# Joined blocks behind the first and third norm of a DeepNorm layer, and an eleventh pair of weights with its sums made ahead

## The chip, the cores and the metric

One core of one Trainium2 chip. The metric is device microseconds (us) from start to end of one execution. The trace is that of one profiled execution; its times are us from the start of its span. TensorE is PE, VectorE is DVE, ScalarE is ACT, GpSimd is POOL, SyncE is SP.

## The reference

One layer on 256 tokens of width 2048, all in float32:

```
h = layer_norm(alpha*x + 0.5*swiglu(x, w_ffn1_gu, w_ffn1_down))          # norm i=0
rq, rk, rv, rg, aq, ak, av, gate_r, gate_a = split(h @ w_in)
ret_branch = (silu(rg) * group_norm(retention(rot(rq), rot(rk), rv))) @ w_ret_out
att_branch = sliding_window_attention(rot(aq), rot(ak), av, sinks) @ w_att_out
mixed = (sigmoid(gate_r)*ret_branch + sigmoid(gate_a)*att_branch) @ w_mix_out
h = layer_norm(alpha*h + mixed)                                          # norm i=1
h = layer_norm(alpha*h + 0.5*swiglu(h, w_ffn2_gu, w_ffn2_down))          # norm i=2
ple = sigmoid(h @ w_ple_gate) * (p @ w_ple_proj)
return layer_norm(alpha*h + ple)                                         # norm 3
swiglu(x, w_gu, w_down) = (silu(x @ w_g) * (x @ w_u)) @ w_down           # inner width 5632
```

## The kernel before, in words

**Products.** Every float32 operand is split into a high part (a cast by ScalarE, L105) and a low part (the difference, by VectorE, L106). A product of two such operands is three matmuls: `Sum.add` issues low x high (L431), high x high (L432) and high x low (L433), each with 128 x 128 weights on 512 columns. Weights come from memory in chunks of 512 KB (256 rows of the product by 512 columns): a load on SyncE's queue (L119) into a tile `r...`, then `h...` and `l...`. A chunk gives two k-steps for both halves t of the 128 tokens, 12 matmuls. All these tiles come from one pool of slots. A planner (`plan`, `fill`) keeps a list of the chunks in the order of their use, and loads and splits each as far ahead as slots and a budget of queued TensorE time allow. Each engine, and SyncE's queue, works in the order in which the program was written.

**Units.** A pair of chunks of the two feed-forward products (gate/up) can be worked in several ways, named by a letter in a string per group of 512 columns (`gu_units`, L937): P is plain, 24 matmuls; F is plain with the low part of one of the chunks accumulated by a transfer on POOL's queue (L170); S is a unit of seven products in place of eight, as Strassen's, 21 matmuls, for which VectorE makes four sums (L226 to L229) and three splits; D is the same unit with its sums `u` and `v` made and split ahead and put in memory, from where they are loaded when needed (`Prepared`). `AHEAD` says which pairs of the second feed-forward part are D: ten pairs, in groups 1, 2, 3, 4, 5 and 7.

`sums_ahead` (L275) makes these sums, as a generator: for each pair two loads, four adds on VectorE (L294, L295, L298, L299), two casts on ScalarE (L297, L301), two differences on VectorE (L304, L306) and four stores on SyncE's queue. `run_side` (L366) is called behind each chunk on TensorE: it runs the next job of the list `side` (to which `later(n, job)` adds a job n calls ahead), and one step of the first generator in `slow` and of the first in `lazy`.

**Norm and turn.** Behind each norm the 256 x 2048 result (tiles `f1y`, `mixy`, `f2y`, in four quarters of 512 columns for each half t of the tokens) has to be turned, since the next product needs it by columns (tile `ht`). `ln_turn` does it on TensorE: four 128 x 128 transposes (L693) into `lnps`, a cast (L105) and a difference (L106). `Norm.first` (L809) is called with the first chunks of the next product. It multiplies these for t=0, holding them, and then again for t=1 (this is the held front), while a list of events says after which chunk (counted through both passes) which quarter (t, c) is normalised or turned. Behind the first norm the front is six chunks of block 0 of the retention's values (`rv`), and behind the third, six of block 0 of the embedding's gate (`pg`). The order is written out by hand.

The middle norm does two things otherwise: its front joins two blocks (three pairs of chunks each for both, `FRONT_PAIRS`), and its quarter 3 is turned by a transfer, the class `Turn`: ScalarE copies the quarter's 32-bit words as two planes of 16 bits (`part`, L185), SyncE issues a transposing transfer (`move`, L189), and ScalarE joins the planes again (`join`, L196) before the usual cast and difference. `by_transfer` names the quarters that go this way.

**Stages around the change.** Norm 0; `rv` block 0; features of the retention's queries and keys (`rqk`, L382), beside them the angle tables (`slow`) and the sums ahead; `rv` blocks 1 to 3; `rg`; attention features and, as jobs of `side`, attention (scores L1412, softmax L1417 to L1453, transposing transfers); beside these jobs the four gates `gt`, then the Strassen part of the other gate (`ga0`, `ga1`); the branches, mixing (two more pairs of sums), norm 1, the second feed-forward part, norm 2, the four blocks `pg`, and norm 3 on their sums. Behind each `pg` block `finish` makes the sigmoid (L1632), the product with `ppr` (L1634), the sum with the residual (L1635) and its statistics (L1636).

Of the kernel before, what the change touches and what calls it, by code (L numbers as in the profile page):

```python
# [8 lines left out]
F32 = mybir.dt.float32  # L9
F32R = mybir.dt.float32r  # L10
# [30 lines left out]

SEVEN = (0, 1, 2, 3)

AHEAD = {1: (4, 5), 2: (4,), 3: (4, 5), 4: (4,), 5: (4, 5), 7: (4, 5)}
AHEAD_SLOTS = 36

DELAY = 1
# [15 lines left out]
def layer(ctx: ExitStack, tc: tile.TileContext, io):  # L63
# [13 lines left out]
    def banks(name):  # L77
        return [bank(name + str(j)) for j in range(2)]
# [266 lines left out]
    def take(key):  # L345
        if not ready:
            fill(True)
        u = ready.pop(0)
        assert u.key == key, (u.key, key)
        return u  # L350

    def done(u):
        room["used"] -= u.keeps
        fill()

    def slots_for_weights(n, ahead=45, far=90):
        room.update(slots=n, ahead=ahead, far=far)
# [825 lines left out]
    ret_keys = lambda b: lambda n, p: ("w_ret2", 4 * b + 2 * n, p)  # L1183

    def plan_mixers():
        plan_tokens(("w_rv", 0), KD)
        for grp in range(8):
            plan_features([("w_in_f", grp)], KD)
        for blk in range(1, 4):
            plan_tokens(("w_rv", blk), KD)  # L1190
        for grp in range(8, 16, 2):
            plan_tokens(("w_in_f2", grp), KD)
        plan_tokens(("w_av",), KD, nk=4)
        for grp in (20, 16, 17, 18, 19):
            plan_features([("w_in_f", grp)], KD)
        for grp in range(21, 29, 2):
            plan_tokens(("w_in_f2", grp), KD)
        for b in range(2):
            block_units(GATE_UNITS, gate_keys(b))
        for j in range(0, 8, 2):  # L1200
            plan_tokens(("w_att2", j), KD // 2)
        for b in range(2):
            block_units(RET_UNITS[b], ret_keys(b))
        block_units(MIX_UNITS, mix_keys)
        for blk in range(2, 4):
            plan_tokens(("w_mix", blk), KD)

    def later(n, job):
        for j in range(n):
            if len(side) <= j:  # L1210
                side.append(idle)
        side.insert(n, job)

    def mixers(ht, norm, residual, keepers, away):
# [24 lines left out]
        def values(blk, ps):  # L1239
            hi, lo = (slot([P, 2, 512], F32R, f"rv{w}{blk}") for w in "hl")  # L1240
            for t in range(2):
                split(hi[:, t], lo[:, t], ps[t])
            rv.append((hi, lo))

        ps = banks("rv0")
        sums = [[Sum(ps[t], KD)] for t in range(2)]
        norm.first([(("w_rv", 0, c), 2 * c, 0) for c in range(FRONT)], rhs, sums, (
            (5, (1, 0)), (6, (1, 1)), (8, (1, 2)), (8, "more"), (9, (1, 3)), (10, (0, 3)), (10, "go"),
        ))
        slots_for_weights(24)  # L1250
        for c in range(FRONT, KD // 2):
            u = take(("w_rv", 0, c))
            tokens_chunk(u.chunk, 2 * c, rhs, [sums[t][0] for t in range(2)], (0, 1))
            done(u)
        values(0, ps)
        slots_for_weights(14)
        ahead = [(gu_keys("f2", j)(0, p), gu_keys("f2", j)(1, p)) for j in AHEAD for p in AHEAD[j]]
        def angles():
# [3 lines left out]

        slow.append(angles())
        lazy.append(sums_ahead(ahead[:3], 3, 2))
        lazy.append(sums_ahead(ahead[3:8], 2, 2))
        for grp in range(8):
            ps = banks(f"rqk{grp}")
            features_out([(("w_in_f", grp), ps)], KD, both_halves)
# [2 lines left out]
        decay = [slot([P, 2, 384], F32, f"dec{j}") for j in range(4)]  # L1271
        for j in range(4):
            act.dma_start(decay[j], io["decay"][:, 2 * j : 2 * j + 2, :])
        for blk in range(1, 4):
            ps = banks(f"rv{blk}")
            tokens_out(("w_rv", blk), KD, rhs, ps)
            values(blk, ps)
# [225 lines left out]

        made = {}
        forms = lambda p: made[p // 2](p % 2)
        slots_for_weights(18)
        sig = []
        for j in range(4):
# [76 lines left out]

        lhs = lambda k: of_pairs(mix_t, k)
        slots_for_weights(16)
        lazy.append(sums_ahead(ahead[8:], 3, 2))

        def residual_added(blk, ps):  # L1590
            for t in range(2):
# [33 lines left out]
    def embedding(ht, norm, y):  # L1625
# [36 lines left out]
        def scale(blk):  # L1662
            sl = y[blk][:, 1]
            dve.tensor_tensor(sl, sl, g[blk // 2][:, blk % 2 * 512 : blk % 2 * 512 + 512], ALU.mult)
            v = slot([P, 2, 512], F32R, f"yg{blk}")
            split(v[:, 0], v[:, 1], sl)
            scaled[blk] = v
# [43 lines left out]
                sync.dma_start(out[:, blk * 512 : blk * 512 + 512], sl)  # L1711

        lhs = lambda k: (ht[:, k, :S], ht[:, k, S:])
        for blk in range(4):
            pgs = banks(f"pg{blk}")
            sums = [Sum(b, KD) for b in pgs]
            sg = slot([P, 2, 512], F32, f"sg{blk}")
            key = ("w_pg", blk)
            if blk == 0:
                for j in range(4):  # L1720
                    pp[j] = load_columns(pp, j, "ppr")
                steps = [(key + (c,), 2 * c, 0) for c in range(FRONT)]
                norm.first(steps, lhs, [[s] for s in sums], (
                    (1, (0, 2)), (1, "sums"), (5, (1, 0)), (6, (1, 1)), (7, (1, 2)), (7, "more"), (8, (1, 3)),
                    (9, (0, 3)), (10, "go"),
                ))
                slots_for_weights(24)
                for c in range(FRONT, KD // 2):
                    u = take(key + (c,))
                    tokens_chunk(u.chunk, 2 * c, lhs, sums, (0, 1))  # L1730
                    done(u)
            elif blk < 3:
                for c in range(KD // 2):
                    u = take(key + (c,))
                    tokens_chunk(u.chunk, 2 * c, lhs, sums, (0, 1))
                    done(u)
                    run_side()
            if blk < 3:
                finish(blk, pgs[0], sg, 0)
                later(1, lambda blk=blk, pgs=pgs, sg=sg: finish(blk, pgs[1], sg, 1))  # L1740
                if blk == 0:
                    g, b = ln_vectors(3)
                    two_rows = small.tile([P, 96], F32, tag="plnm", bufs=1, name="plnm")
                    pool.memset(two_rows, 0.0)
                    ident_r = small.tile([P, P], F32R, tag="identr", bufs=1, name="identr")
                    act.copy(ident_r, ident)
                if blk == 1:
                    later(3, rows_of_vectors)
                    later(4, lambda: scale(0))
                    later(6, lambda: scale(1))  # L1750
                if blk == 2:
                    later(6, lambda: scale(2))
# [55 lines left out]
    with tc.manual_schedule():  # L1808
        dve.memset(warm, 0.0)
        for eps, v in roots.items():  # L1810
            dve.memset(v, 4.0 * eps)
        act.activation(warm, warm, AF.Silu)
        plan_ffn("f1")
        plan.extend(Single(("w_pp", blk, 0)) for blk in range(2))
        plan_mixers()
        plan.extend(Single(("w_pp", blk, 0)) for blk in range(2, 4))
        plan_ffn("f2")
        for blk in range(4):
# [108 lines left out]
```

## Time and profile before

| what | us |
|---|---|
| median of three runs | 2230.26 (2229.8 to 2233.0) |
| the profiled execution, its own time | 2231.88 |
| its span, first to last instruction | 2230.0 |
| TensorE busy | 2220.2 |
| VectorE busy | 1999.0 |
| ScalarE busy | 1429.3 |

The granted TensorE clock is 0.999 on average. A row of the timeline has start, duration, engine, line, operation, output <- inputs and in brackets the idle time ahead of it with what ended it; rows of the same line in succession are put together (x4). A row of the windows has the stretch, its length, for each engine its busy time and instructions, and at the end the granted clock, the mean share of the DMA engines and GB/s. A group has its busy time and mean ns behind the bar. Matmuls overlap, so the duration of one (390 ns) is no price; the distance between the starts is.

### The profile page before, as it was taken

The numbers are of one execution on the slowest core, as the hardware profiler recorded it, in microseconds if no ns is written. First come the engines' busy times: TensorE is split into PE (matmuls) and PEld (weight loads), VectorE is DVE, ScalarE is ACT, GpSimd is POOL, SyncE is SP. The second block draws the span as 40 slices with busy tenths as digits, with TensorE's granted clock in tenths as the row PEclk, the third lists the DMA queues.
The fourth block names the chain that finished last, engine by engine and source line by source line (L and its number), as shares of the span: only waits on it lengthen the run. The fifth ranks groups of instructions, "written<-read, shape, count | busy, mean of one in ns | idle before, by whom it ended". The sixth has DMA issues, their size and how long they took to land.

```text
span 2230.0 us, 29094 instructions
## 1 busy us (share of the span) xinstructions
PE 2220.2 (100%) x10159; PEld 1841.2 (83%) x10159; DVE 1999.0 (90%) x2619; ACT 1429.3 (64%) x1670; POOL 51.9 (2%) x66
## 2 busy tenths in 40 slices
PE   9999999999999999999999999999999999999998
PEld 8888888888888888888788888888888888888887
DVE  6999999989988898889789888779999999999977
ACT  6777777776565445557766467466667677765633
POOL 0000000000000000000000000000000000000000
PEclk9999999999999999999999999999999999999999
DMA  9989998976686989846756578788898999676871
GB/s 323 254 259 257 250 258 249 263 225 217 230 306 255 324 297 320 268 172 208 208 166 240 176 210 323 302 302 274 304 299 269 297 249 276 205 237 224 300 272 68
DMA packets 296363, 565.01 MB, mean 253 GB/s; under 512 B 94348, under 2 KB 98828, under 8 KB 296216
## 3 DMA queue, kind: packets, MB, share of 16 engines
q1 hardware_dynamic: 286024, 530.68, 71.3%
q0 software_dynamic: 8208, 29.89, 7.2%
q10 hardware_dynamic: 1984, 2.58, 0.3%
q8 instruction: 80, 1.31, 0.2%
q14 instruction: 67, 0.55, 0.1%
HBM read 484.43 MB, written 29.36 MB: 230 GB/s over the span
## 4 chain that ended last, share of the span: by engine, by line
PE 94%; DVE 2%; DMA 2%; issue 1%; ACT 0%; SPq 0%; ACTq 0%; POOL 0%; DVEq 0%; POOLq 0%
PE f2g L432 3%; PE f2g L431 3%; PE f2g L433 3%; PE rqk L382 3%; PE f1g L433 2%; PE f1g L431 2%; PE f1g L432 2%; PE f2u L432 2%; PE f2u L431 2%; PE f2u L433 2%; PE f1u L433 2%; PE f1u L431 2%; PE f1u L432 2%; PE aqk L382 2%; PE f2e L431 1%; PE f2e L432 1%
## 5 line engine op out<-in xcount | busy, mean ns | idle before, releaser
L106 DVE TENSOR_TENSOR lf_gu<-rf_gu,hf_gu 128x1024 fp32r<-128x1024 f32 (+1 forms) x225 | 267.6, 1210 | 23.7 <-ACT hf_gu L105 22.7
L105 ACT CAST hf_gu<-rf_gu 128x1024 fp32r<-128x1024 f32 (+1 forms) x225 | 228.6, 1039 | 25.8 <-DMA rf_gu<-in_f_gu 21.8
L106 DVE TENSOR_TENSOR lw_in_f<-rw_in_f,hw_in_f 128x1024 fp32r<-128x1024 f32 x140 | 167.6, 1219 | 18.6 <-ACT hw_in_f L105 18.4
L106 DVE TENSOR_TENSOR lf_down<-rf_down,hf_down 128x1024 fp32r<-128x1024 f32 x130 | 155.7, 1219 | 14.1 <-ACT hf_down L105 13.3
L105 ACT CAST huf_gu<-uf_gu 128x1024 fp32r<-128x1024 f32 x76 | 80.1, 1054 | 122.7 <-DVE uf_gu L227 104.0
L105 ACT CAST hf_down<-rf_down 128x1024 fp32r<-128x1024 f32 x130 | 132.6, 1048 | 31.2 <-DMA rf_down<-in_f_down 21.3
L105 ACT CAST hw_in_f<-rw_in_f 128x1024 fp32r<-128x1024 f32 x140 | 140.9, 1049 | 9.0 <-DMA rw_in_f<-in_w_in_f 4.0
L105 ACT CAST hvf_gu<-vf_gu 128x1024 fp32r<-128x1024 f32 x76 | 80.1, 1054 | 31.6 <-DVE vf_gu L229 29.3
L106 DVE TENSOR_TENSOR luf_gu<-uf_gu,huf_gu 128x1024 fp32r<-128x1024 f32 x76 | 92.6, 1218 | 0.0
L106 DVE TENSOR_TENSOR lvf_gu<-vf_gu,hvf_gu 128x1024 fp32r<-128x1024 f32 x76 | 92.5, 1218 | 0.0
L431 PE MATMUL f1g<-hf_gu,xt 128*128 128x512 f32 x232 | 90.7, 391 | 0.0
L432 PE MATMUL f1g<-hf_gu,xt 128*128 128x512 f32 x232 | 90.5, 390 | 0.0
L433 PE MATMUL f1g<-lf_gu,xt 128*128 128x512 f32 x232 | 90.4, 390 | 0.0
L431 PE MATMUL f2g<-hf_gu,ht 128*128 128x512 f32 x214 | 83.3, 389 | 0.0
L433 PE MATMUL f2g<-lf_gu,ht 128*128 128x512 f32 x214 | 83.3, 389 | 0.0
L432 PE MATMUL f2g<-hf_gu,ht 128*128 128x512 f32 x214 | 83.3, 389 | 0.0
L170 POOL DMA_DIRECT2D lf_gu<-rf_gu x43 | 37.4, 869 | 1640.7 <-PE f2u L433 980.9
L433 PE MATMUL f1u<-lf_gu,xt 128*128 128x512 f32 x192 | 74.9, 390 | 0.5 <-DMA lf_gu<-rf_gu 0.5
L431 PE MATMUL f1u<-hf_gu,xt 128*128 128x512 f32 x192 | 74.7, 389 | 0.0
L432 PE MATMUL f1u<-hf_gu,xt 128*128 128x512 f32 x192 | 74.7, 389 | 0.0
L105 ACT CAST huf_down<-uf_down 128x1024 fp32r<-128x1024 f32 x32 | 33.7, 1053 | 60.0 <-DVE uf_down L227 58.7
L431 PE MATMUL f2u<-hf_gu,ht 128*128 128x512 f32 x168 | 65.6, 391 | 0.0
(1498 smaller groups left out, 6921.5 us busy)
## 6 DMA issues: line engine op xcount, KB each, us to landing
rf_gu<-in_f_gu SPq DMA_DIRECT2D x360, 512.0 KB
rf_down<-in_f_down SPq DMA_DIRECT2D x176, 512.0 KB
rw_in_f<-in_w_in_f SPq DMA_DIRECT2D x148, 512.0 KB
lf_gu<-rf_gu POOLq DMA_DIRECT2D x43, 512.0 KB, 7.9
rw_rv<-in_w_rv SPq DMA_DIRECT2D x32, 512.0 KB
rw_ret<-in_w_ret SPq DMA_DIRECT2D x32, 512.0 KB
rw_mix<-in_w_mix SPq DMA_DIRECT2D x32, 512.0 KB
rw_pg<-in_w_pg SPq DMA_DIRECT2D x32, 512.0 KB
```

What stands on the lines that cost most here:

```text
L105: act.copy(dst_hi, src)
L106: (lo_engine or dve).tensor_tensor(dst_lo, src, dst_hi, ALU.subtract)
L170: pool.dma_start(c.lo, c.raw, accum_op=ALU.add)
L382: pe.matmul(ps[f], hi[:, kk, f * P : (f + 1) * P], rhs(k), start=k == 0, stop=k == n_k - 1,)
L431: pe.matmul(o, al, bh, start=first, stop=False)
L432: pe.matmul(o, ah, bh, start=False, stop=False)
L433: pe.matmul(o, ah, bl, start=False, stop=self.left == 0)
```

## The change

1. `AHEAD` gets `6: (4,)`: group 6 of the second feed-forward part goes from `PFSSFSSP` to `PFSSDSSP`. Eleven pairs have their sums made ahead: three and then three (five before) beside `rqk`, `rv` and `rg`, three in the gates (new), two in the mixing as before.
2. Behind norm 0, blocks 0 and 1 of `rv` are joined: the held front is three pairs of chunks for both blocks, the other five pairs follow with `run_side` behind each chunk, and block 1 no longer comes behind `rqk`.
3. Behind norm 2, blocks 0 and 1 of `pg` are joined in the same way. Their finishes become jobs of `side` in block 2, and the preparations for norm 3 (`rows_of_vectors`, `scale`) go behind them.
4. At both places quarter 3 is turned by a transfer and joined by a job of `side`, one call behind the front; the lists of events are written anew.

```
-AHEAD = {1: (4, 5), 2: (4,), 3: (4, 5), 4: (4,), 5: (4, 5), 7: (4, 5)}
+AHEAD = {1: (4, 5), 2: (4,), 3: (4, 5), 4: (4,), 5: (4, 5), 6: (4,), 7: (4, 5)}
...
-        ps = banks("rv0")
-        sums = [[Sum(ps[t], KD)] for t in range(2)]
-        norm.first([(("w_rv", 0, c), 2 * c, 0) for c in range(FRONT)], rhs, sums, (
-            (5, (1, 0)), (6, (1, 1)), (8, (1, 2)), (8, "more"), (9, (1, 3)), (10, (0, 3)), (10, "go"),
-        ))
+        pv = [banks(f"rv{n}") for n in range(2)]
+        sums = [[Sum(pv[n][t], KD) for n in range(2)] for t in range(2)]
+        norm.by_transfer = 3,
+        norm.first(
+            [(("w_rv", n, p), 2 * p, n) for p in range(FRONT_PAIRS) for n in range(2)], rhs, sums, (
+                (5, (1, 0)), (6, (1, 1)), (7, (1, 2)), (7, "more"), (8, (0, 3)), (8, (1, 3)), (9, ("move", 3)), (10, "go"),
+            )
+        )
+        later(1, lambda: norm.join(3))
         slots_for_weights(24)
-        for c in range(FRONT, KD // 2):
-            u = take(("w_rv", 0, c))
-            tokens_chunk(u.chunk, 2 * c, rhs, [sums[t][0] for t in range(2)], (0, 1))
-            done(u)
-        values(0, ps)
+        for p in range(FRONT_PAIRS, KD // 2):
+            for n in range(2):
+                u = take(("w_rv", n, p))
+                tokens_chunk(u.chunk, 2 * p, rhs, [sums[t][n] for t in range(2)], (0, 1))
+                done(u)
+                run_side()
+        for blk in range(2):
+            values(blk, pv[blk])
...
         lazy.append(sums_ahead(ahead[:3], 3, 2))
-        lazy.append(sums_ahead(ahead[3:8], 2, 2))
+        lazy.append(sums_ahead(ahead[3:6], 2, 2))
...
-        for blk in range(1, 4):
+        for blk in range(2, 4):
             ps = banks(f"rv{blk}")
...
+        lazy.append(sums_ahead(ahead[6:9], 2, 2))
         slots_for_weights(18)
...
-        lazy.append(sums_ahead(ahead[8:], 3, 2))
+        lazy.append(sums_ahead(ahead[9:], 3, 2))
...
+        norm.first(
+            [(("w_pg", n, p), 2 * p, n) for p in range(FRONT_PAIRS) for n in range(2)], lhs, sums, (
+                (1, "sums"), (4, (0, 2)), (5, (1, 0)), (6, (1, 1)), (7, "more"), (8, (1, 2)), (8, (0, 3)), (9, (1, 3)), (10, ("move", 3)), (10, "go"),
+            )
+        )
+        later(1, lambda: norm.join(3))
...
+        for blk in range(2):
+            finish_later(2 * blk, blk, pair[blk], gates[blk])
...
+        later(4, rows_of_vectors)
+        later(5, lambda: scale(0))
+        later(6, lambda: scale(1))
```

The order of the instructions shows what moves. First TensorE at the end of the held front behind norm 0, before (`rv01` is block 0 for t=1, `lnps0112` and `lnps0012` are quarter 3 for t=1 and t=0):

```order
L433 MATMUL rv01_6129<-lw_rv_0_2_5900,ht0_5955 128x512
L693 MATMUL lnps0112_6228<-ident_72,f1y3_5591 128x128 x4
L431 MATMUL rv01_6129<-hw_rv_0_3_5917,ht0_5955 128x512
L432 MATMUL rv01_6129<-hw_rv_0_3_5917,ht0_5955 128x512
L433 MATMUL rv01_6129<-lw_rv_0_3_5918,ht0_5955 128x512
```

The same place of the change, behind the last group of transposes that is left (quarter 2 for t=1, `lnps018`; `rv11` is block 1 for t=1):

```order
L433 MATMUL rv01_6129<-lw_rv_0_0_5864,ht0_5955 128x512
L693 MATMUL lnps018_6209<-ident_72,f1y2_5545 128x128 x4
L431 MATMUL rv11_6131<-hw_rv_1_0_5881,ht0_5955 128x512
L432 MATMUL rv11_6131<-hw_rv_1_0_5881,ht0_5955 128x512
L433 MATMUL rv11_6131<-lw_rv_1_0_5882,ht0_5955 128x512
```

Both groups of quarter 3 are gone, quarter 2's group stands behind the first held chunk of the second pass and not behind a later one, and each chunk alternates with one of block 1. In all TensorE has 16 transposes and 3 matmuls fewer.

ScalarE at the end of the same front, before (`hw_rv_0_6` is the high part of chunk 6 of block 0):

```order
L105 CAST ht0_5955<-lnps018_6213 128x4x128
L105 CAST ht0_5955<-lnps0112_6228 128x4x128
L105 CAST ht0_5955<-lnps0012_6241 128x4x128
L105 CAST hw_rv_0_6_6254<-rw_rv_0_6_5952 128x1024
L105 CAST hw_rv_0_7_6258<-rw_rv_0_7_5962 128x1024
```

And of the change (`wln03`, `mln03` and `lnr03` are quarter 3 as planes, turned, and joined; `few` is a table's first use):

```order
L105 CAST ht0_5955<-lnps018_6209 128x4x128
L185 COPY wln03_6224<-f1y3_5591 128x1024 x2
L105 CAST hw_rv_0_3_6247<-rw_rv_0_3_5952 128x1024
L105 CAST hw_rv_1_3_6251<-rw_rv_1_3_5962 128x1024
L105 CAST hw_rv_0_4_6255<-rw_rv_0_4_6054 128x1024
...
L671 ACT_TABLE_LOAD
L671 ACTIVATE few_81<-few_81 128x1
L196 COPY lnr03_6314<-mln03_6233 128x2x4x128 x2
L105 CAST ht0_5955<-lnr03_6314 128x4x256
L105 CAST hw_rv_0_7_6359<-rw_rv_0_7_6170 128x1024
```

Two casts of `lnps` have become two copies ahead of eight casts of weights, and the join stands behind the table load, ahead of the casts for the last pair.

VectorE in the gates, before (`lw_in_f2_21_7` is the low part of chunk 7 of the first gate, `asm2` and `asc2` are a softmax's sums and scores, `attt0` the attention's result, split):

```order
L1453 TENSOR_SCALAR asc2_9590<-asc2_9590,asm2_9654 128x256 x2
L106 TENSOR_TENSOR lw_in_f2_21_7_9696<-rw_in_f2_21_7_9569,hw_in_f2_21_7_9695 128x1024
L106 TENSOR_TENSOR lw_in_f2_23_0_9717<-rw_in_f2_23_0_9630,hw_in_f2_23_0_9716 128x1024
L1489 TENSOR_TENSOR attt0_9577<-ao10_9722,attt0_9577 64x256
L1489 TENSOR_TENSOR attt0_9577<-ao11_9723,attt0_9577 64x256
```

And of the change (L1460 and L1496 are the L1453 and L1489 of before):

```order
L1460 TENSOR_SCALAR asc2_9534<-asc2_9534,asm2_9602 128x256 x2
L294 TENSOR_TENSOR uf2_gu_5_0_4_9631<-rf2_gu_5_0_4_9576,rf2_gu_5_1_4_9578 128x512
L295 TENSOR_TENSOR uf2_gu_5_0_4_9631<-rf2_gu_5_1_4_9578 128x512
L106 TENSOR_TENSOR lw_in_f2_21_7_9656<-rw_in_f2_21_7_9513,hw_in_f2_21_7_9655 128x1024
L106 TENSOR_TENSOR lw_in_f2_23_0_9677<-rw_in_f2_23_0_9574,hw_in_f2_23_0_9676 128x1024
L1496 TENSOR_TENSOR attt0_9521<-ao10_9682,attt0_9521 64x256
L1496 TENSOR_TENSOR attt0_9521<-ao11_9683,attt0_9521 64x256
```

The first two adds of the sums for a pair of group 5 stand ahead of the low parts for the gates; the other adds and the differences follow in the same way, for three pairs.

More of the change, by code (lines that the diff above doesn't have):

```diff
@@ L1185, in plan_mixers @@
     def plan_mixers():
-        plan_tokens(("w_rv", 0), KD)
+        block_units([("P", p) for p in range(KD // 2)], lambda n, p: ("w_rv", n, p))
         for grp in range(8):
             plan_features([("w_in_f", grp)], KD)
-        for blk in range(1, 4):
+        for blk in range(2, 4):
             plan_tokens(("w_rv", blk), KD)
@@ L1273, in mixers @@
             act.dma_start(decay[j], io["decay"][:, 2 * j : 2 * j + 2, :])
-        for blk in range(1, 4):
+        for blk in range(2, 4):
             ps = banks(f"rv{blk}")
@@ L1713, in embedding, with finish_later @@
         lhs = lambda k: (ht[:, k, :S], ht[:, k, S:])
-        for blk in range(4):
+        def finish_later(n, blk, pgs, sg):
+            later(n, lambda: finish(blk, pgs[0], sg, 0))
+            later(n + 1, lambda: finish(blk, pgs[1], sg, 1))
+        pair = [banks(f"pg{blk}") for blk in range(2)]
+        sums = [[Sum(pair[n][t], KD) for n in range(2)] for t in range(2)]
+        gates = [slot([P, 2, 512], F32, f"sg{blk}") for blk in range(2)]
+        for j in range(4):
+            pp[j] = load_columns(pp, j, "ppr")
+        norm.by_transfer = 3,
+        norm.first(
[4 more added lines that the diff above has]
+        later(1, lambda: norm.join(3))
+        slots_for_weights(24)
+        for p in range(FRONT_PAIRS, KD // 2):
+            for n in range(2):
+                u = take(("w_pg", n, p))
+                tokens_chunk(u.chunk, 2 * p, lhs, [sums[t][n] for t in range(2)], (0, 1))
+                done(u)
+                run_side()
+        for blk in range(2):
+            finish_later(2 * blk, blk, pair[blk], gates[blk])
+        g, b = ln_vectors(3)
+        two_rows = small.tile([P, 96], F32, tag="plnm", bufs=1, name="plnm")
+        pool.memset(two_rows, 0.0)
+        ident_r = small.tile([P, P], F32R, tag="identr", bufs=1, name="identr")
+        act.copy(ident_r, ident)
+        later(4, rows_of_vectors)
+        later(5, lambda: scale(0))
+        later(6, lambda: scale(1))
+        for blk in range(2, 4):
             pgs = banks(f"pg{blk}")
@@ L1718, in embedding @@
             key = ("w_pg", blk)
[L1719 to L1732, printed above, removed]
+            if blk == 2:
                 for c in range(KD // 2):
@@ L1737, in embedding @@
                     run_side()
-            if blk < 3:
                 finish(blk, pgs[0], sg, 0)
                 later(1, lambda blk=blk, pgs=pgs, sg=sg: finish(blk, pgs[1], sg, 1))
[L1741 to L1752, printed above, removed]
+                later(6, lambda: scale(2))
                 continue
@@ L1817, in layer @@
         plan_ffn("f2")
-        for blk in range(4):
+        block_units([("P", p) for p in range(KD // 2)], lambda n, p: ("w_pg", n, p))
+        for blk in range(2, 4):
             plan_tokens(("w_pg", blk), KD)
```

## The prediction

> **What bounds the kernel now.** I read the page first: how busy each engine is, its granted clock, and the chain of work that ended last.
>
> ```profile
> PE 2220.2 (100%) x10159; PEld 1841.2 (83%) x10159; DVE 1999.0 (90%) x2619; ACT 1429.3 (64%) x1670; POOL 51.9 (2%) x66
> PEclk9999999999999999999999999999999999999999
> PE 94%; DVE 2%; DMA 2%; issue 1%; ACT 0%; SPq 0%; ACTq 0%; POOL 0%; DVEq 0%; POOLq 0%
> ```
>
> TensorE (PE) is busy for 2220.2 of 2230.0 us at full granted clock and makes 94% of the chain. A busy TensorE could still be a waiting one, so the list of its waits comes next.
>
> ```profile
> PE warm L1806 <- POOL ident masks.py:199: 1.4, 1, 1.4
> PE f1e L431 <- DVE evw L550: 0.7, 1, 0.7
> PE mr1a L433 <- DVE lw_ret L106: 0.5, 1, 0.5
> PE f1u L433 <- DMA lf_gu<-rf_gu: 0.5, 2, 0.3
> ...
> ```
>
> The four rows left out are 0.3 and three of 0.2, so the whole list is about 4.0 us, 1.4 of them before the first matmul of the layer. So the kernel is bound by what TensorE has to issue, and the price of a matmul is the distance between two starts. Two windows, each from the start of one block of the embedding's gate to the next (96 matmuls), give it:
>
> ```profile
> 2152.37:2174.13 21.76, 21.76 (x97) 18.02 (x96) 13.13 (x14) 8.86 (x12) 1.48 (x2) 1.00 0.57 191
> 2174.13:2195.89 21.76, 21.76 (x97) 18.02 (x96) 17.80 (x20) 11.32 (x15) 0.00 (x0) 1.00 0.22 80
> ```
>
> 21.76 / 96 = 0.2267 us. Time is won only by taking instructions off TensorE, and lost only where VectorE (DVE), ScalarE (ACT) or a transfer comes too late for it.
>
> **What TensorE loses.** Group 6 turns a pair of four products (24 matmuls) into a unit of seven (21): 3 x 0.2267 = **0.68 us**. The two norms lose quarter 3's transposes, four groups of four. Rows of TensorE behind the third norm, one group after every six matmuls:
>
> ```profile
> 2136.75 0.60 PE L693 MATMUL lnps<-ident,f2y 128*128 128x128 f32 x4
> 2138.58 0.60 PE L693 MATMUL lnps<-ident,f2y 128*128 128x128 f32 x4
> 2140.42 0.60 PE L693 MATMUL lnps<-ident,f2y 128*128 128x128 f32 x4
> 2142.34 0.63 PE L693 MATMUL lnps<-ident,f2y 128*128 128x128 f32 x4
> ```
>
> The first two spacings are 1.83 and 1.84; less 6 x 0.2267 = 1.36, a group costs 0.47, and four cost **1.88 us**. The last spacing is 1.92, so 0.09 more goes with the wait of that last group, which is one of those removed. Joining two blocks by itself changes no count: the same chunks are multiplied in another order.
>
> One row gives each transpose a longer span:
>
> ```profile
> L693 PE MATMUL lnps<-ident,f1y x32: 270/272/275, 688.3 to 711.0; 128*128 128x128 f32 x32
> ```
>
> At its own 272 ns, sixteen would be 4.35 us; but groups of four that add 0.47 show that they overlap, and I count 1.88. The Trainium skill's TensorE: Matmul & The Clock Gate, Part 4: PE-mode transpose, gives about 275 ns in a kernel's context, which this row matches as a span; counted as issue time it would make the sum an estimated 2.5 us better, and the spacing speaks against that.
>
> **What the first norm adds.** ScalarE now copies quarter 3 into 16-bit words (two L185 copies) ahead of the first new weights, and SyncE issues the turning transfer. Rows of VectorE and TensorE before:
>
> ```profile
> 708.26 0.69 DVE L106 TENSOR_TENSOR ht<-lnps,ht 128x512 fp32r<-128x512 f32 x1 [1.06 <-ACT ht L105]
> 709.65 0.75 DVE L681 SCALAR_TENSOR_TENSOR f1y<-f1y,rstd,ln_b 128x512 f32<-128x512 f32 x1
> 713.85 0.39 PE L431 MATMUL rv<-hw_rv,ht 128*128 128x512 f32 x1
> ```
>
> The middle norm already works this way, so its rows price the new steps (ScalarE, VectorE, SyncE):
>
> ```profile
> 1462.53 1.99 ACT L185 COPY wln<-mixy 128x1024 uint16<-128x1024 uint16 x2 [0.38 <-DVE mixy L681]
> 1464.43 7.70 ACT L105 CAST hf_gu<-rf_gu 128x1024 fp32r<-128x1024 f32 x8
> 1472.15 1.28 ACT L671 ACT_TABLE_LOAD   x1
> 1473.55 2.56 ACT L196 COPY lnr<-mln 128x1024 uint16<-128x1024 uint16 x2
> 1476.14 1.05 ACT L105 CAST ht<-lnr 128x1024 fp32r<-128x1024 f32 x1
> 1477.22 1.23 DVE L106 TENSOR_TENSOR ht<-lnr,ht 128x1024 fp32r<-128x1024 f32 x1 [2.54 <-ACT ht L105]
> 1464.55 1.78 SPq L189 DMA_TRANSPOSE mln<-wln  x1
> ```
>
> TensorE is through its held chunks at 713.85 before; with two groups fewer at 713.85 - 0.94 = 712.91. It then needs the first new weight's high part, and its low part two matmuls later, at 713.37. Quarter 3's last row ends at 710.40 before; quarter 2's transposes now come one step earlier, which removes the 1.06 idle at 708.26: 709.34. Then the copies (1.99), one cast (1.05) and one subtract (1.23): 713.6, so TensorE waits **0.25 us**. If the idle does not go, it is 1.3; if the copies overlap the rows' seams, nothing. I take 0.25, since the earlier transposes are in the order.
>
> Quarter 3 itself: copies done at 711.33, eight casts (7.70), table load and its activation (1.4), join (2.56), cast (1.05), subtract (1.23) give about 725.3. TensorE wants it after six chunks of 12 matmuls, 16.32 us: at about 729.4. Four us are spare, so I cost the join at nothing; the cover is those six chunks.
>
> **What the third norm adds.** The same, from these rows of VectorE and TensorE:
>
> ```profile
> 2141.44 0.75 DVE L681 SCALAR_TENSOR_TENSOR f2y<-f2y,rstd,ln_b 128x512 f32<-128x512 f32 x1
> 2146.93 0.39 PE L431 MATMUL pg<-hw_pg,ht 128*128 128x512 f32 x1
> ```
>
> The weight at 2146.93 (the first that was not held) is now due at 2146.93 - 0.94 - 0.09 = 2145.90, its low part at 2146.36. Quarter 3 ends at 2142.19 at the latest, plus 1.99 + 1.05 + 1.23 = 2146.46: a wait of **0.1 us**, bounds 0 and 1 (one more cast in front). The finishes of blocks 0 and 1 move into block 2. Each half is three VectorE steps of about 0.7 us; block 0's two halves add 4.3 us to block 2's 17.80, which makes 22.1 in 21.76. Bounds: nothing, since VectorE had 8.6 us idle in the block before and can run its subtracts ahead there, or the whole 4.3. I take nothing.
>
> **What the gates add.** Three pairs of sums are made beside the gates instead of beside the features. What three pairs cost VectorE, from the groups of the features' stage; then, as windows, that stage, the gates up to their Strassen part, and a piece of that part:
>
> ```profile
> L306 DVE TENSOR_TENSOR lvf_gu<-vf_gu,hvf_gu 128x1024 fp32r<-128x1024 f32 x3 | 3.7, 1219 | 0.0
> L304 DVE TENSOR_TENSOR luf_gu<-uf_gu,huf_gu 128x1024 fp32r<-128x1024 f32 x3 | 3.7, 1218 | 0.0
> ...
> L299 DVE TENSOR_TENSOR vf_gu<-vf_gu,rf_gu 128x512 f32<-128x512 f32 x3 | 2.1, 692 | 0.1
> ```
>
> ```profile
> 719.30:808.70 89.40, 89.40 (x514) 78.68 (x513) 79.62 (x119) 42.37 (x58) 0.00 (x0) 1.00 0.86 303
> 1044.00:1150.00 106.00, 106.00 (x523) 83.22 (x523) 82.95 (x154) 78.08 (x140) 0.00 (x0) 1.00 0.65 195
> 1165.00:1180.00 15.00, 15.00 (x68) 12.43 (x67) 14.90 (x17) 10.86 (x13) 0.00 (x0) 1.00 0.57 213
> ```
>
> The other three adds are of L299's shape, so three pairs are 3.7 + 3.7 + 4 x 2.1 = 15.8 us. VectorE is idle for 106.00 - 82.95 = 23.05 us of the gates, so they would leave 7.2: 93% busy, against 89% beside the features, where such sums cost TensorE no wait in the list. The DMA share is 0.65 against 0.86. How far weights run ahead there (VectorE's subtract, then the first matmul that reads it, by counting chunks), and the tightest place behind the gates:
>
> ```profile
> 1121.44 1.22 DVE L106 TENSOR_TENSOR lw_in_f<-rw_in_f,hw_in_f 128x1024 fp32r<-128x1024 f32 x1
> 1175.59 1.22 DVE L106 TENSOR_TENSOR lvw_in_f<-vw_in_f,hvw_in_f 128x1024 fp32r<-128x1024 f32 x1
> ```
>
> ```profile
> 1129.91 0.39 PE L433 MATMUL gt<-lw_in_f,ht 128*128 128x512 f32 x1
> 1177.62 0.39 PE L433 MATMUL ga0s<-lvw_in_f,gaf1h 128*128 128x512 f32 x1
> ```
>
> 7.3 us ahead in the gates, 0.8 in the Strassen part. I cost the sums at **nothing**: the idle time covers them. Group 6's unit replaces one transfer by POOL and loads what was stored; group 4 has it at the same place already without a row in the wait list, so nothing again. The two pairs taken from the features free an engine that held nobody up.
>
> **Sum.** -0.68 - 1.88 - 0.09 + 0.25 + 0.1 = -2.3 us. The profiled execution took 2231.88 (span 2230.0 and 1.9 around it), so it would take 2229.6. The median of the runs shown, 2230.26, lies 1.6 below the profiled one: **2228.0**. That is 0.1%; a measurement of this kernel can tell about 0.2% (4.5 us) from no change.
>
> **Rivals.**
> (a) *VectorE's queue in the gates becomes the bound (slower).* An add of the sums (L294) that waits for its loads holds every subtract and softmax step queued behind it, so idle time next to it may not be usable. With usable idle U of the 23 us, 15.8 - U of backlog reaches the Strassen part, where VectorE is busy 14.90 of 15 us and catches nothing up, and 0.8 are spare: TensorE waits 15.0 - U. A half usable (11.5) gives 3.5 us and 2231.5, a sixth (4) gives 11.0 and 2239.0; the point beyond which it is slower by over 0.2% (2234.7, so 6.7 us of wait) is U under 8.3. For it: VectorE takes its queue in order, and the gates' idle time is itself partly waits. Against it: 0.1 idle before L299 beside the features, and 9.8 us of idle were left there with more DMA load.
> (b) *The turned quarter lands late at the first norm.* The transfer stands behind loads, in this state of the DMA engines (share in the last columns), against the middle norm's:
>
> ```profile
> 714.00:724.00 10.00, 10.00 (x50) 8.38 (x49) 9.24 (x10) 9.82 (x12) 0.00 (x0) 1.00 1.03 407
> 1464.50:1474.00 9.50, 9.50 (x44) 7.86 (x43) 8.49 (x8) 9.47 (x12) 0.00 (x0) 1.00 0.92 280
> ```
>
> The middle join began 9.0 us after the issue (1464.55 to 1473.55), at once behind the table's activation. ScalarE reaches the join here at about 720.4, 9 us after the issue too, and 4.2 are spare. Landing after 18 us, twice as long, makes TensorE wait 4.8: 2232.8, which is no change by the bound. ScalarE's later casts stand behind the join as well.
> The Trainium skill's VectorE: DVE Perf Modes, The three transpose paths, gives 1309 ns for a 128x128 transpose by DMA of 16-bit data. A quarter is 16 of these, an estimated 20.9 us one after another, and the wait would be an estimated 7.7 us; the middle norm's transfer turns a quarter of the same size within 9.0 us, so the trace disagrees and (b) gets no larger chance by it.
> (c) *The gain is eaten:* 1.3 at the first norm, 1 at the third: 2229.9. The same 2 us and more would go if the finishes in block 2 held up the last weights.
> (d) *The change does not do what it says:* the order shows four groups of transposes and three matmuls fewer, so this cannot be.
>
> **How the numbers follow.** Forecast (2226.5 to 2229.2) 0.60; (c) 0.16; (b) with a wait of 1 to 5 us 0.08; (a) with U under 8.3, beyond the bound, 0.12; faster by over 0.2% would need 2.1 of the 4.0 us of listed waits to vanish as well, 0.04. So faster 0.04, within 0.2% 0.84, slower 0.12. The range runs from 2226.4 (no new wait, and a us of scatter) to 2232.8 (case b).
>
> **What would show it.** Right: transposes of f1y and f2y count 24 each; first new weights at 712.9 to 713.4 and 2145.9 to 2146.5 on their norms' clocks; ScalarE's L196 joins begin without a wait for the transfer; no TensorE wait on gt or ga0 rows. Wrong: a wait of TensorE for lw_in_f, lvw_in_f, apt or ht in the list, a VectorE idle before L294, or a group spacing that gives less than 0.47 back.

## The result, and the profile after

The changed kernel takes 2229.21 us (median of 22 runs, 2226.47 to 2230.62) where the kernel before takes 2231.78 (22 runs, 2229.8 to 2233.87; three of them gave the 2230.26 shown above). The ratio is 0.9987, with a 95% interval of 0.9982 to 0.9993: 2.6 us or 0.13% faster, between 1.6 and 4.0 us. That is less than the 0.2% that was called no change, and clear of zero.

The busy line and the chain of the page after, in the columns of before:

```profile
PE 2218.5 (100%) x10140; PEld 1838.9 (83%) x10140; DVE 2004.0 (90%) x2624; ACT 1439.0 (65%) x1677; POOL 50.9 (2%) x65
...
PE 93%; DMA 3%; DVE 2%; issue 1%; ACT 0%; SPq 0%; ACTq 0%; POOL 0%; DVEq 0%; POOLq 0%
```

TensorE has 19 instructions fewer and is 1.7 us less busy; VectorE and ScalarE have 5 and 10 us more to do. The list of TensorE's waits after (three rows of 0.2 left out):

```profile
PE warm L1822 <- POOL ident masks.py:199: 1.4, 1, 1.4
PE f1u L433 <- DMA lf_gu<-rf_gu: 1.2, 2, 0.9
PE f1e L431 <- DVE evw L550: 0.6, 1, 0.6
PE mr1a L433 <- DVE lw_ret L106: 0.5, 1, 0.5
PE f2e L431 <- DVE evw L550: 0.5, 1, 0.5
```

Nothing of `rv`, `gt`, `ga0` or `pg` stands in it. The waits for `lf_gu` and `evw` lie in code that the change does not touch, and they come and go: the first `rv` starts anywhere from 693.64 to 696.34 in the 13 profiles of this document, all with the same code in front of it. So stages are compared by the distance between two starts of TensorE in one execution. First the six landmarks before (first `rv`, `rg`, `f26s`, `f27s`, `pg`, `pln`), then after:

```profile
695.17 0.39 PE L431 MATMUL rv<-hw_rv,ht 128*128 128x512 f32 x1
...
873.97 0.39 PE L431 MATMUL rg<-hw_in_f,ht 128*128 128x512 f32 x1
...
1705.55 0.39 PE L431 MATMUL f26s<-hf_gu,ht 128*128 128x512 f32 x1
...
1746.35 0.39 PE L431 MATMUL f27s<-hf_gu,ht 128*128 128x512 f32 x1
...
2127.60 0.40 PE L431 MATMUL pg<-hw_pg,ht 128*128 128x512 f32 x1
...
2217.66 0.40 PE L1673 MATMUL pln<-yg,identr 128*128 128x512 f32 x1
```

```profile
696.34 0.39 PE L431 MATMUL rv<-hw_rv,ht 128*128 128x512 f32 x1
...
874.55 0.39 PE L431 MATMUL rg<-hw_in_f,ht 128*128 128x512 f32 x1
...
1705.82 0.39 PE L431 MATMUL f26s<-hf_gu,ht 128*128 128x512 f32 x1
...
1745.94 0.39 PE L431 MATMUL f27s<-hf_gu,ht 128*128 128x512 f32 x1
...
2127.77 0.40 PE L431 MATMUL pg<-hw_pg,ht 128*128 128x512 f32 x1
...
2216.94 0.40 PE L1681 MATMUL pln<-yg,identr 128*128 128x512 f32 x1
```

| stage, us | before | after | difference | predicted |
|---|---|---|---|---|
| first norm: rv to rg | 178.80 | 178.21 | -0.59 | -0.94 + 0.25 = -0.69 |
| gates: gt to ma | 180.39 | 180.38 | 0 | 0 |
| group 6: f26s to f27s | 40.80 | 40.12 | -0.68 | -0.68 |
| third norm: pg to pln | 90.06 | 89.17 | -0.89 | -0.94 - 0.09 + 0.1 = -0.93 |
| sum | | | -2.16 | -2.30 |

The first `gt` starts at 1046.42 before and 1047.00 after, the first `ma` at 1226.81 and 1227.38. The small remainder to the measured 2.6 lies inside its interval of 1.6 to 4.0.

The two small waits, too short for the list above, first behind norm 0 (ScalarE, VectorE, SyncE, TensorE), then behind norm 2 (VectorE, TensorE), all after:

```profile
710.50 1.99 ACT L185 COPY wln<-f1y 128x1024 uint16<-128x1024 uint16 x2 [2.48 <-DVE f1y L681]
...
721.52 2.54 ACT L196 COPY lnr<-mln 128x1024 uint16<-128x1024 uint16 x2
709.66 0.75 DVE L681 SCALAR_TENSOR_TENSOR f1y<-f1y,rstd,ln_b 128x512 f32<-128x512 f32 x1
713.48 3.50 DVE L106 TENSOR_TENSOR lw_rv<-rw_rv,hw_rv 128x1024 fp32r<-128x1024 f32 x3 [3.07 <-ACT hw_rv L105]
...
725.18 1.23 DVE L106 TENSOR_TENSOR ht<-lnr,ht 128x1024 fp32r<-128x1024 f32 x1 [2.52 <-ACT ht L105]
712.52 2.03 SPq L189 DMA_TRANSPOSE mln<-wln  x1
714.07 0.39 PE L431 MATMUL rv<-hw_rv,ht 128*128 128x512 f32 x1
714.30 0.39 PE L432 MATMUL rv<-hw_rv,ht 128*128 128x512 f32 x1
714.76 0.50 PE L433 MATMUL rv<-lw_rv,ht 128*128 128x512 f32 x1
715.10 0.39 PE L431 MATMUL rv<-hw_rv,ht 128*128 128x512 f32 x1
...
730.77 0.39 PE L431 MATMUL rv<-hw_rv,ht 128*128 128x512 f32 x1
```

```profile
2145.25 6.90 DVE L106 TENSOR_TENSOR lw_pg<-rw_pg,hw_pg 128x1024 fp32r<-128x1024 f32 x6 [2.41 <-ACT hw_pg L105]
2146.25 0.39 PE L432 MATMUL pg<-hw_pg,ht 128*128 128x512 f32 x1
2146.53 0.50 PE L433 MATMUL pg<-lw_pg,ht 128*128 128x512 f32 x1
2146.87 0.39 PE L431 MATMUL pg<-hw_pg,ht 128*128 128x512 f32 x1
```

At 714.76 TensorE waits for the first new low part: the step from 714.30 is 0.46 in place of 0.23, and the next one is 0.34, so the wait costs another 0.11 behind itself. That is 0.35 for a forecast of 0.25; the same pattern (steps of 0.28 and 0.34) costs 0.17 at 2146.53, for 0.1. Quarter 3 is complete at 726.41 (725.18 and 1.23) and first read 72 matmuls behind 714.07, at 730.77: 4.4 us spare, for a forecast of 4.

### The profile page after: what moved, and what is told of

Its sections match the earlier page's. It is cut to its first block, busy times and chain, and to the rows that moved or that the text cites. A ratio compares the mean times of both kernels' runs of the same rounds, so it can differ in the third digit from the quotient of the medians.

```text
span 2228.6 us, 29103 instructions
## 1 busy us (share of the span) xinstructions
PE 2218.5 (100%) x10140; PEld 1838.9 (83%) x10140; DVE 2004.0 (90%) x2624; ACT 1439.0 (65%) x1677; POOL 50.9 (2%) x65
## 4 chain that ended last, share of the span: by engine, by line
PE 93%; DMA 3%; DVE 2%; issue 1%; ACT 0%; SPq 0%; ACTq 0%; POOL 0%; DVEq 0%; POOLq 0%
PE rqk L382 3%; PE f2g L431 3%; PE f2g L433 3%; PE f2g L432 3%; PE f1g L431 2%; PE f1g L433 2%; PE f1g L432 2%; PE f2u L431 2%; PE f2u L433 2%; PE f2u L432 2%; PE f1u L433 2%; PE f1u L431 2%; PE f1u L432 2%; PE aqk L382 2%; PE f2e L431 1%; PE f1e L431 1%
## 5 line engine op out<-in xcount | busy, mean ns | idle before, releaser
L1057 ACT ACTIVATE eve<-eve 128x1024 f32<-128x1024 f32 x20 | 21.2, 1061 | 67.3 <-DVE eve L1056 67.3
```

Source lines behind the costliest of these rows:

```text
L1057: act.activation(g, g, AF.Silu)
```

## The experiments

Differences of tenths of a us are below what the times tell, so verdicts here rest on stage distances, and the times stand beside them. All were worked out as in the table above.

**1. The kernel before, once more.**

> The kernel before, unchanged, profiled a second time, as the measure of scatter. Theory A (the change saves what TensorE no longer issues, at the spacing of its starts) compares distances between two starts of TensorE in one execution; it needs them to repeat: first rv matmul to first rg matmul 178.80 us, first f26s to first f27s 40.80, first pg to first pln 90.06, each within 0.1 us. The start of rv itself (695.17) may move by about 1 us, since the changed kernel reached it 1.17 later with the same code in front. Rival B (the stages differ by such scatter, and the gain is not where A puts it): the three distances differ by 0.5 or more.

178.83, 40.80 and 90.01 (2232.11 us, one run); `rv` starts 0.14 earlier than in the first profile. The distances repeat within 0.05, so -0.59, -0.68 and -0.89 are not scatter. The changed code repeats nearly as well: in the changed kernel and the seven kernels below that keep both of its norms, rv to rg is 178.20 to 178.27, pg to pln 89.14 to 89.30.

**2. Joined blocks, quarter 3 turned on TensorE.** At both places:

```
-        norm.by_transfer = 3,
-        later(1, lambda: norm.join(3))
 (first norm)
-(7, (1, 2)), (7, "more"), (8, (0, 3)), (8, (1, 3)), (9, ("move", 3)), (10, "go"),
+(8, (1, 2)), (8, "more"), (9, (1, 3)), (10, (0, 3)), (10, "go"),
 (third norm)
-(7, "more"), (8, (1, 2)), (8, (0, 3)), (9, (1, 3)), (10, ("move", 3)), (10, "go"),
+(7, (1, 2)), (7, "more"), (8, (1, 3)), (9, (0, 3)), (10, "go"),
```

> The changed kernel, but quarter 3 turned on TensorE at both norms, by the events of before; the blocks stay joined. Theory A: joining in itself is worth nothing, and the 16 transposes cost 4 x 0.47. First rv to first rg 178.8 (178.21 with the transfer: 0.94 more for two groups, 0.23 less for the wait of the first new weight, which goes), first pg to first pln 90.0 to 90.1 (89.17 with the transfer); the median 1.5 to 1.6 us above the changed kernel. Rival B (joining gives the gain, since weights of two blocks run further ahead): both distances stay at 178.2 and 89.2.

First norm 178.80, exactly as before: joining alone is worth nothing there, the transposes carry the gain. Third norm 90.51, 0.45 more than before, which was not expected; the median is 2231.18 against 2231.37, a ratio of 0.9998 (0.9989 to 1.0007). Groups of transposes there, in that kernel:

```profile
2136.20 0.60 PE L693 MATMUL lnps<-ident,f2y 128*128 128x128 f32 x4
2138.11 0.66 PE L693 MATMUL lnps<-ident,f2y 128*128 128x128 f32 x4
2140.25 0.63 PE L693 MATMUL lnps<-ident,f2y 128*128 128x128 f32 x4
2142.30 0.63 PE L693 MATMUL lnps<-ident,f2y 128*128 128x128 f32 x4
```

They are 1.91, 2.14 and 2.05 apart in place of 1.83: TensorE waits at each for VectorE's next normalised quarter (the groups start 0.05, 0.15 and 0.15 us behind the end of VectorE's row), since quarter 2 of t=0 was moved from event 1 to event 4: VectorE's subtract for it starts at 2133.81 in that kernel and at 2130.24 in the kernel before, so that the quarters behind it come later. So at the third norm the transfer also takes away waits that this list of events would have brought.

**3. The eleventh pair alone**, in the kernel before:

```
-..., 5: (4, 5), 7: (4, 5)}
+..., 5: (4, 5), 6: (4,), 7: (4, 5)}
-        lazy.append(sums_ahead(ahead[3:8], 2, 2))
+        lazy.append(sums_ahead(ahead[3:6], 2, 2))
+        lazy.append(sums_ahead(ahead[6:9], 2, 2))      (ahead of the gates)
-        lazy.append(sums_ahead(ahead[8:], 3, 2))
+        lazy.append(sums_ahead(ahead[9:], 3, 2))
```

> The kernel before with the eleventh pair alone: group 6 with a unit of stored sums, and the sums made three, three, three and two. Theory A: first f26s to first f27s 40.12 (40.80 before), the gates (first gt to first ma) 180.4 as before, nothing else moves; median 0.7 us below before. Rival (the gates pay for it: VectorE's queue late): the gates' distance grows by 0.3 or more, up to the 0.68 gained.

Group 6 takes 40.12, the gates 180.38, the norms 178.79 and 90.02; 2230.19 us, ratio 0.9995 (0.9986 to 1.0004). So this part of the gain does not hang on the other two.

**4. The transfer without joined blocks**, behind the first norm of the kernel before:

```
+        norm.by_transfer = 3,
         norm.first([(("w_rv", 0, c), 2 * c, 0) for c in range(FRONT)], rhs, sums, (
-            (5, (1, 0)), (6, (1, 1)), (8, (1, 2)), (8, "more"), (9, (1, 3)), (10, (0, 3)), (10, "go"),
+            (5, (1, 0)), (6, (1, 1)), (7, (1, 2)), (7, "more"), (8, (0, 3)), (8, (1, 3)), (9, ("move", 3)), (10, "go"),
         ))
+        norm.join(3)
```

> The kernel before with quarter 3 turned by the transfer behind the first norm only, block 0 alone as before, so that the chunks which read quarter 3 come right behind the held front. Theory A with its cover (joining is there to hide the way of quarter 3 over ScalarE and the transfer, ready about 12 us after the front ends): TensorE waits 11 to 13 us for ht, and first rv to first rg grows from 178.8 to about 190. Rival B (the transfer is short enough to need no joined blocks): a wait under 3 us, and the distance stays under 181.

2243.68 us. rv to rg is 192.13, 13.33 more than before. Its list of waits, and four windows around the wait (the granted clock is the third number from the end):

```profile
PE rv L431 <- DVE ht L106: 12.2, 1, 12.2
```

```profile
712.00:714.60 2.60, 0.20 (x1) 0.00 (x0) 2.60 (x3) 2.60 (x4) 0.00 (x0) 1.00 1.14 254
714.60:724.30 9.70, 0.00 (x0) 0.00 (x0) 7.25 (x7) 8.38 (x9) 0.00 (x0) 0.50 1.02 375
724.30:728.30 4.00, 3.94 (x9) 3.14 (x10) 0.00 (x0) 0.00 (x0) 0.00 (x0) 0.50 1.04 420
728.30:731.00 2.70, 2.70 (x13) 2.19 (x12) 0.00 (x0) 0.00 (x0) 0.00 (x0) 1.00 0.26 99
```

The wait is as long as the way of quarter 3. This is what the joined blocks are for: not a gain, but 16 us of matmuls that do not read it. And the wait costs more than itself: 2.4 us into it (712.2 to 714.6) the clock falls to half, and stays there for 3.9 us of matmuls, another 2.0. 12.2 + 2.0 - 0.94 (the transposes) is 13.3.

The Trainium skill's TensorE: Matmul & The Clock Gate, Why this matters for your kernels, asks for no idle gaps over about 3 us and for 4 us or more of continuous work to reach full rate. This trace agrees with the second, with 3.9 us; the first is too generous here, since the clock fell 2.4 us into this wait, and in experiment 7 behind waits of 1.8 and 2.0 us.

**5. The transfer later on SyncE's queue.** First behind the event that releases the loads:

```
-(8, (1, 3)), (9, ("move", 3)), (10, "go"),
+(8, (1, 3)), (10, "go"), (12, ("move", 3)),
```

> The changed kernel with the transposing transfer behind the first norm issued at the end of the front, behind the loads that the planner lets go there, in place of ahead of them. Case b of the prediction: SyncE issues up to nine loads of 512 KB first (6.5 us of issue, 11 us of transfer at 420 GB/s), so the quarter lands 7 to 11 us later than in the changed kernel, where it was ready 4.2 us ahead of TensorE: TensorE waits 3 to 7 us for ht and first rv to first rg is 181 to 185. Rival (the transfer overtakes loads on other engines, or the planner issues few there): under 1 us, 178.2 to 179.

No effect (178.27; 2228.24 us), but the edit moved nothing either: SyncE's rows have the same order as in the changed kernel (six loads of `rv`, the transfer, four stores, nine loads), and the transfer's issue begins 0.02 us behind the end of the copies, 0.03 in the changed kernel. Then by a call behind the front:

```
-(8, (1, 3)), (9, ("move", 3)), (10, "go"),
+(8, (1, 3)), (10, "go"),
...
+        later(0, lambda: norm.turns[3].move())
         later(1, lambda: norm.join(3))
```

> The changed kernel with the transposing transfer behind the first norm issued by the first call behind the front: on SyncE's queue it stands behind the four stores of the normalised rows (3.2 us of issue) and the loads that the planner lets go with the first chunk. Case b of the prediction, now with something in front: the join waits 4 to 9 us for the transfer, 4.2 are spare, so TensorE waits 0 to 5 us for ht; a wait of over 4 us should also lower the granted clock as it did without joined blocks. First rv to first rg 178.2 to 184. Rival (transfers of SyncE's queue run beside one another, the order does not matter): 178.2.

ScalarE's and SyncE's rows in that kernel:

```profile
720.51 2.56 ACT L196 COPY lnr<-mln 128x1024 uint16<-128x1024 uint16 x2 [1.28 <-DMA mln<-wln]
710.15 8.33 SPq L189 DMA_TRANSPOSE mln<-wln  x1
```

The join now does wait, 1.28 us, until 10.4 us behind the start of the issue, and TensorE does not (178.20; 2228.27 us): the spare time takes it. The four stores stand ahead of the transfer now, but they were issued by 708.4, and the transfer's issue again began 0.02 us behind the copies. What grew is the row of the issue, 8.33 us in place of 2.03; why is not shown. No load got ahead of the transfer in either kernel, and one that lands 5 us late was not brought about, so what case (b) would cost was not tried.

**6. More pairs.** Thirteen and twelve, in the changed kernel:

```
-..., 6: (4,), 7: (4, 5)}
+..., 6: (4,), 7: (4, 5), 8: (4,), 10: (4,)}      (thirteen: 3, 5, 3 and 2 at a time)
+..., 6: (4,), 7: (4, 5), 8: (4,)}                (twelve: 3, 4, 3 and 2)
```

> The changed kernel with two pairs more, in groups 8 and 10 (thirteen), their sums made five beside the features, rv and rg as before the change, three in the gates, two in the mixing and the first three as now. Theory A: each pair takes 0.68 off its group: first f28s to f29s 40.12 (40.80 in the changed kernel) and first f210s to first f2d shorter by 0.68; median 1.4 us below the changed kernel. Rival (the stored sums' loads or VectorE come late in the later groups, which have a pair accumulated by POOL beside them): waits for lvf_gu, hvf_gu or their loads in TensorE's list take it back, 0 to 1.4 us.

> The changed kernel with one pair more, in group 8 (twelve), its sums made beside rv and rg. Theory A: first f28s to first f29s 40.12 as with thirteen pairs, and group 10, which lost 2.5 us there, back at 29.92; gates 180.38; median 0.7 us below the changed kernel, which is under what the times can tell. Rival (group 10 lost because the transfers of all later groups are late): first f210s to first f2d over 30.5.

Thirteen: group 8 drops to 40.12, but group 10 to the next stage grows from 29.92 to 32.45; 2230.66 us, ratio 0.9995 (0.9986 to 1.0004). Its waits, and VectorE at that place:

```profile
PE f210s L433 <- DVE lf_gu L106: 1.4, 1, 1.4
...
PE f210s L433 <- DVE luf_gu L106: 0.8, 1, 0.8
```

```profile
1876.22 0.69 DVE L226 TENSOR_TENSOR uf_gu<-rf_gu,rf_gu 128x512 f32<-128x512 f32 x1 [3.26 <-DMA rf_gu<-in_f_gu]
```

VectorE idles 3.26 us for a load, then works without a gap up to TensorE's waits, and TensorE waits for it. Twelve: group 8 at 40.12 and group 10 at 29.92, as expected, but group 9 at 41.90 for 40.80, with a wait of 0.8 for `lf_gu`, POOL's transfer. That kernel takes 2228.26 us, ratio 0.9986 (0.9977 to 0.9995), which cannot be told apart from the changed kernel's 0.9987 (0.9982 to 0.9993). Whether group 9 always pays is open, since it was profiled once, and waits for the same kind of transfer come and go in the first feed-forward part (0 to 1.2 us in the 13 profiles).

**7. What the gates can take.** Six pairs of sums there, a step at every chunk:

```
-        lazy.append(sums_ahead(ahead[3:6], 2, 2))
-        lazy.append(sums_ahead(ahead[6:9], 2, 2))
+        lazy.append(sums_ahead(ahead[3:9], 2, 1))      (ahead of the gates)
```

> The changed kernel with six pairs of sums in the gates in place of three, a step at every chunk, and only the first three beside the features. 31.6 us of VectorE work for 23 us of its idle time there. Theory A with all idle time usable: the backlog is 8.6 us, 0.8 is spare in the Strassen part, so TensorE waits about 8 us for lw_in_f, lvw_in_f or the attention between first gt and first ma (180.4 to about 188). Rival (only half the idle time is usable, case a of the prediction with U at 11.5): about 19 us, 199. If weights run far enough ahead everywhere: nothing, 180.4.

2244.89 us; gt to ma 197.80, 17.4 more, near the rival's 19. But it is not that rival. TensorE's waits, and two windows, the DMA share next to the end:

```profile
PE ao L1487 <- ACT apt L201: 6.4, 2, 6.0
PE gt L433 <- DVE lw_in_f L106: 4.2, 4, 2.7
```

```profile
1100.00:1120.00 20.00, 17.36 (x79) 12.10 (x77) 17.67 (x32) 13.81 (x24) 0.00 (x0) 1.00 1.06 363
1120.00:1140.00 20.00, 15.09 (x67) 11.66 (x68) 16.74 (x30) 13.75 (x24) 0.00 (x0) 0.83 1.07 375
```

VectorE is idle for 2.3 and 3.3 us of these windows, while the DMA engines are full. A pair is not only 5.3 us of VectorE, but 1 MB of loads and 2 MB of stores. So two theories were set against each other: VectorE's work of six pairs with the transfers of three (each VectorE instruction of the three pairs issued twice, by a loop around it), and the reverse (six more stores of 512 KB for each pair, to memory that nothing reads).

> The changed kernel with each of the six VectorE instructions of the three pairs made in the gates issued twice: VectorE's work of six pairs, transfers of three. Theory V (VectorE's queue is what six pairs broke, as case a says): gates (first gt to first ma) 188 or more. Theory D (it was the DMA engines, whose share was 1.0 to 1.08 when six pairs were made, and VectorE idle 2 to 3 us of 20 while TensorE waited): under 183, since VectorE's work only fits in.

> The changed kernel with six more stores of 512 KB for each of the three pairs made in the gates: transfers of six pairs, VectorE's work of three. Theory D: the DMA engines are full, the attention's transposing transfers land late, TensorE waits for apt as with six pairs: gates 185 to 198. Theory V: 180.4, since VectorE does nothing more.

VectorE twice: gt to ma 191.02, +10.6 (2237.58 us). More stores: 195.75, +15.4 (2243.15 us). One wait and one window of each, VectorE twice first:

```profile
PE gt L439 <- DVE lw_in_f L106: 5.6, 4, 2.0
```

```profile
1120.00:1140.00 20.00, 16.19 (x62) 12.61 (x63) 19.56 (x35) 13.36 (x24) 0.00 (x0) 0.91 0.68 210
```

```profile
PE ao L1494 <- ACT apt L201: 10.6, 2, 6.4
```

```profile
1100.00:1120.00 20.00, 15.83 (x78) 12.18 (x76) 15.59 (x28) 12.81 (x25) 0.00 (x0) 1.00 1.09 369
```

Neither theory alone holds. Either work breaks the gates when doubled, each by its own way: VectorE's (19.56 of 20 busy, DMA share 0.68) through late low parts, the transfers (DMA share 1.09, VectorE 15.59) through the attention's transposing transfer, for which ScalarE's `apt` and then TensorE's `ao` wait. SyncE's and ScalarE's rows of one such transfer, with more stores:

```profile
1108.14 5.79 SPq L189 DMA_TRANSPOSE mat<-wat  x1
1118.09 1.95 ACT L201 COPY apt<-mat 128x768 uint16<-128x768 uint16 x2 [5.38 <-DMA mat<-wat]
```

Its issue begins 0.02 us behind the copies of its words, so it did not stand unissued behind the stores; but the row of the issue lasts 5.79 us, where the changed kernel's six of the gates last 1.4 to 2.2, and ScalarE waits 5.38 us for the transfer. Whether the full DMA engines hold it up, or the queue that it shares with the stores, was not separated. With six pairs, both doubled, the loss is 17.4, not 26: they overlap, though that kernel also makes a step at every chunk and not at every second one. The changed kernel itself, at 1044 to 1150:

```profile
1044.00:1150.00 106.00, 106.00 (x525) 83.34 (x525) 96.26 (x171) 83.32 (x146) 0.00 (x0) 1.00 0.91 284
```

In this window VectorE went from 82.95 to 96.26, and the DMA share from 0.65 to 0.91. Three pairs fit, and both resources are about nine tenths used.

## Why the prediction was right, step by step

- **What bounds the kernel, and the price of an instruction.** Right. Each of the three stages with fewer instructions became shorter by what the spacing gave, and the same 0.94 showed in the opposite direction in experiment 2 (178.21 back to 178.80, with the wait of 0.35 gone). Counting 272 ns for each transpose would have asked for more than twice that.
- **The waits for the first new weights.** The mechanism was right, the sizes a little small: 0.35 and 0.17 for 0.25 and 0.1, since the restart behind a wait costs another 0.11 that the working left out. The 0.17 that they cost beyond the forecast accounts for the difference between -2.30 and -2.16.
- **The join at no cost.** Right, with 4.4 us spare for 4; experiment 4 shows the price without its cover, 13.3 us.
- **The finishes in block 2 at no cost.** pg to pln contains them and shows no wait: -0.89 leaves no room for one.
- **The sums in the gates at no cost.** Right in outcome, and shown by experiment 3 for itself. The working was incomplete: it weighed VectorE's idle time, and passed over the DMA share with a remark that 0.65 is below 0.86. Doubled, the transfers cost more (+15.4) than VectorE's work (+10.6). Case (a)'s formula gives 7.8 us for VectorE's doubled work with all idle time usable (31.6 - 23.05 - 0.8); 10.6 were measured, of which 5.6 are in the list; in two windows of lowered clock, the one shown and 1140 to 1150 at 0.83, an estimated 3.5 more went (20 x 0.09 + 10 x 0.17). The rest is not accounted for. The sign that the prediction named for (a) did not show: VectorE has no listed idle time ahead of any of its eleven L294 rows after the change.
- **Joining in itself at no cost.** Right at the first norm. At the third, the new list of events without the transfer costs 0.45, which the sum never saw, since both came together.
- **The turned quarter lands late, case (b).** It did not happen: the join at 721.52 has no idle time ahead of it. What it would cost was not tried (experiment 5).
- **The time.** 2228.0 was forecast from a median of three runs that lay 1.5 us below that of 22; the forecast difference, -2.3, met -2.6 with its interval. By the number alone, 2229.21 lies a hair above the forecast's own band (2226.5 to 2229.2) and nearer to case (c), 2229.9; but the waits of (c), 1.3 and 1 us, did not occur (0.35 and 0.17). The low base made the miss, not the mechanism.

## What to carry to other kernels

Where one engine is always busy, count the instructions it loses, price them by the distance of their starts, and find for each moved step the stretch of work that hides it; when that stretch is missing, the wait can cost several times the gain. Before work is put into a stage's idle time, look at every resource that it uses, the transfers with it: an engine's idle share says nothing of the DMA engines. And compare stages by landmarks within one execution when the sought difference is smaller than the scatter of the whole.

## What the runs showed of the hardware

- TensorE's clock fell to 0.50 of full speed 2.4 us into a wait of 12.2 us, and came back 3.9 us after work began again, so that a long wait cost 2.0 us more than its length. Shorter waits also lowered it: with VectorE's work twice, to 0.50 for 3.4 us at a time, from 1120.5 and from 1141.0, 0.3 and 1.4 us behind the end of waits of 1.8 and 2.0 us; behind the wait of 1.6 us between them (it ended at 1134.6) the clock stayed at 1.00 until 1141.0. In the four kernels with such waits every stretch at 0.50 in the gates and behind the first norm lasted 3.4, 6.8 or 13.7 us, steps of 3.4.
- A wait of 0.23 us for a low part (714.76) cost TensorE 0.35, since the step behind it was 0.34 in place of 0.23.
- A transposing transfer of one quarter (two planes of 16 bits) was done within 9.0 us of the start of its issue in the changed kernel, 712.52 to the join at 721.52, with a DMA share of 1.04 (714 to 724), and within 10.4 us with four stores issued ahead of it.
- Four transposes of 128 x 128 float32 in a row, each 272 ns long in the trace, add 0.47 us between the matmuls around them.
